# The first of seven products in one 512-column matmul per weight block, in the 12 pairs that follow a Down

## The chip, the cores and the metric

The kernel runs on one core of one Trainium2 chip. The metric is device time in microseconds (us) of one execution. A core has five engines with queues of their own: PE (matmuls; its weight loads are listed as PEld), DVE (elementwise work on vectors), ACT (activations and copies), POOL and SP (here, for the most part, issuing DMAs). PE writes its sums into PSUM banks; ACT and DVE read them from there into SBUF.

## The reference

A decoder trunk of two layers on 512 tokens of width 1024, in f32. Per layer:

```python
h = x + 0.5 * swiglu(rms_norm(x, ffn1_norm[l]), ffn1_w1[l], ffn1_w3[l], ffn1_w2[l])
n = rms_norm(h, mix_norm[l])
p = n @ w_in[l]          # conv, sliding-window attention, memory attention
h = h + y @ w_out[l]
h = h + 0.5 * swiglu(rms_norm(h, ffn2_norm[l]), ffn2_w1[l], ffn2_w3[l], ffn2_w2[l])
x = rms_norm(h, final_norm[l])
```

with `swiglu(x, w1, w3, w2) = (silu(x @ w1) * (x @ w3)) @ w2` and an inner width of 2816, that is 22 blocks of 128 columns. So there are four feed-forward blocks, and the change is in the `x @ w1` and `x @ w3` of each of them.

## The kernel before, in words

**Precision.** An f32 operand is split in two parts, hi (rounded to the format that PE multiplies) and lo (what is left). A product of two f32 operands is three products of parts: weight hi by operand hi, weight hi by operand lo, weight lo by operand hi. The split of a weight tile is one ACT copy to `whi` (line 148) and one DVE subtraction to `wlo` (line 149); there are four buffers of each.

**ffn** (from line 512 on) makes one feed-forward block. The 22 column blocks of w1 and w3 are worked in four quarters, `QUARTERS = ((0, 6), (6, 6), (12, 6), (18, 4))`. In each quarter `up_pair` is called for column blocks two by two (f, f + 1), and one pair of the next quarter is made ahead; then comes the quarter's *Down*: for each of the eight blocks of the output width, matmuls of lines 180 to 182 with w2 into a bank named `mm`, and a DVE instruction of line 611 that adds it to `h`. The pairs f = 0 and 2 are made without up_pair; f = 4 is `PLAIN`, f = 6 the last branch of up_pair, and f = 8 to 20 take the branch `full`. So each quarter but the first begins, behind the Down of the quarter before, with a pair f = 8, 14 or 20; f = 10, 12 and 16, 18 follow another pair.

**up_pair** (line 363) makes a pair's two column blocks, for w1 and w3 (i = 0, 1), by a Strassen-like scheme: the contraction of 1024 is cut in two halves, the tokens in two halves of 256 (`QT`), and instead of eight products of halves there are seven (numbered j = 1 to 7), of sums of weight halves with sums of operand halves. The operand sums stand ready as `M.m[j][k]`, each a tile of 128 x 2 x 256 with hi and lo side by side. The weight tiles are `raw[i]` as loaded, `raw[i]` after two sums on DVE (line 402), `X[i]` (named `wsum`, summed by an accumulating DMA on POOL, line 372) and `z`; each is split by `unit` before use.

A product has two forms.

- `product` (line 378, matmuls on line 383): for each of four contraction blocks a matmul of 256 columns with hi and one with lo, all into the same 256 columns of a bank, then four of 256 with weight lo: 12 matmuls. The whole product stands in one half of the bank.
- `beside` (line 386, matmuls on line 391): hi and lo in one matmul of 512 columns, into the two halves of a bank, then four of 256 with weight lo into the first half: 8 matmuls. The product is the sum of the bank's halves.

In the branch `full`, `x[i]` is a bank named `pt`. Products 1, 6 and 5 go into it one on top of the other, and after each the running sum is taken to `part[i]`. For products 6 and 5 this is done by the helper `both`: `beside`, a copy of the bank's first half by ACT (line 440), and an add of its second half by DVE (line 402, `part <- part, pt`). Product 1 has the form `product`, and ACT alone takes it to `part` (line 446). Product 2 goes into a bank `po` by `beside`; `summed` adds its two halves to `part` on DVE. Products 3 (bank `cf` or `mm`), 7 and 4 (banks `po`) have the form `beside` too.

**Order.** The instructions' order on each engine is not that of the program: a planner places each by its priority and a modelled due time, allocates the buffers and sets the waits. `tc.issue_after` holds an instruction back until another is issued. Once planned, the order on an engine is fixed, and an instruction whose input is late holds what is behind it.

Of the kernel before, what the change touches and what calls it, by code (L numbers as in the profile page):

```python
# [65 lines left out]
def trunk(ctx: ExitStack, tc: tile.TileContext, xT, memT, pos, w1a, w3a, w2a, w1b, w3b, w2b,  # L66
# [293 lines left out]
        unit.at = split(p[0], p[1], x, V)[1]  # L360
        return p

    def up_pair(l, w13, f, M, full, behind=None):

        raw = [raw_tile(w13[i][l, f], D) for i in range(2)]
        X = []
        for i in range(2):

            x = wst.tile([P, UNIT], F32, tag="aux", name="wsum", bufs=3)
            with tc.issue_after(behind.ins) if behind else nullcontext():  # L370
                nc.sync.dma_start(x.rearrange("p (f c) -> p f c", f=2), w13[i][l, f : f + 2, :, 0:QW].rearrange("f p c -> p f c"))
            G.dma_start(x, w13[i][l, f + 1], accum_op=ALU.add)
            X.append(x)
        z = wst.tile([P, UNIT], F32, tag="raw", name="raw", bufs=3)
        for i in range(2):
            nc.sync.dma_start(z[:, blk(i, QW)], w13[i][l, f + 1, :, QW:])
        x0, x1 = blk(0, QT), blk(1, QT)

        def product(ps, w, half, j, first=False):


            for n, (part, q) in enumerate([(0, q) for k in range(4) for q in ((k, 0), (k, 1))] + [(1, (k, 0)) for k in range(4)]):
                tail[0] = T.matmul(ps, w[part][:, blk(4 * half + q[0])], M.m[j][q[0]][:, q[1]], skip_group_check=True,  # L383
                                   start=first and not n, stop=n == 11)

        def beside(ps, w, half, j, first=False):


            def go(out, part, n):
                for k in range(4):  # L390
                    tail[0] = T.matmul(out, w[part][:, blk(4 * half + k)], M.m[j][k][:, 0:n], skip_group_check=True,  # L391
                                       start=first and not part and k == 0, stop=part == 1 and k == 3)

            go(ps, 0, 2)
            go(ps[:, 0], 1, 1)

        u, g = (tmp.tile([P, 2, S], F32, tag=t, name=t, bufs=n) for t, n in (("u", 1), ("g", 2)))
        part = [tm("part", "sq", 2) for _ in range(2)]
        to = (u, g)

        def add(out, a, b):
            V.tensor_tensor(out=out, in0=a, in1=b, op=ALU.add)

        def summed(out, ps, a):
            add(out, ps[:, 0], a)
            add(out, out, ps[:, 1])

        if f == PLAIN:
            xy = [bank([P, S], "po") for _ in range(2)]
            zv = [bank([P, S], "pt") for _ in range(2)]  # L410
            for i in range(2):
                w = unit(raw[i])
                product(xy[i][:, x0], w, 0, 1, first=True)
                product(xy[i][:, x1], w, 1, 2)
                A.activation(part[i], xy[i], AF.Copy)
                add(to[i][:, 0, x0], part[i][:, x0], part[i][:, x1])

                add(raw[i][:, 0:QW], raw[i][:, 0:QW], X[i][:, QW:])
                add(raw[i][:, QW:], raw[i][:, QW:], raw[i][:, 0:QW])
            for i in range(2):  # L420
                w = unit(raw[i])
                product(xy[i][:, x0], w, 0, 6)
                A.activation(part[i][:, x1], xy[i][:, x0], AF.Copy)
                product(zv[i][:, x0], w, 1, 3, first=True)
            for i in range(2):
                w = unit(X[i])
                product(xy[i][:, x0], w, 1, 5)
                A.activation(part[i][:, x0], xy[i][:, x0], AF.Copy)
                product(zv[i][:, x1], w, 0, 7)
                add(to[i][:, :, x1], zv[i].rearrange("p (n t) -> p n t", n=2), part[i][:, x0].unsqueeze(1).to_broadcast([P, 2, QT]))  # L430
            w = unit(z)
            for i in range(2):
                product(zv[i][:, x1], w, i, 4)
                add(to[i][:, 1, x0], zv[i][:, x1], part[i][:, x1])
        elif full:
            x = [bank([P, 2, QT], "pt") for _ in range(2)]

            def both(i, w, half, j, t, first=False):
                beside(x[i], w, half, j, first)
                A.activation(part[i][:, t], x[i][:, 0], AF.Copy)  # L440
                add(part[i][:, t], part[i][:, t], x[i][:, 1])

            for i in range(2):
                w = unit(raw[i])
                product(x[i][:, 0], w, 0, 1, first=True)
                A.activation(part[i][:, x0], x[i][:, 0], AF.Copy)
                y = bank([P, 2, QT], "po")
                beside(y, w, 1, 2, first=True)
                summed(to[i][:, 0, x0], y, part[i][:, x0])
            c, v = [bank([P, 2, QT], t) for t in ("cf", "mm")], []  # L450
            for i in range(2):
                with tc.issue_after(unit.at.ins):
                    add(raw[i][:, 0:QW], raw[i][:, 0:QW], X[i][:, QW:])
                add(raw[i][:, QW:], raw[i][:, QW:], raw[i][:, 0:QW])
                w = unit(raw[i])
                both(i, w, 0, 6, x1)
                beside(c[i], w, 1, 3, first=True)
                w = unit(X[i])
                v.append(bank([P, 2, QT], "po"))
                beside(v[i], w, 0, 7, first=True)  # L460
                A.activation(to[i][:, 1, x1], v[i][:, 0], AF.Copy)
                add(to[i][:, 1, x1], to[i][:, 1, x1], v[i][:, 1])
                both(i, w, 1, 5, x0)
                summed(to[i][:, 0, x1], c[i], part[i][:, x0])
                add(to[i][:, 1, x1], to[i][:, 1, x1], part[i][:, x0])
            w = unit(z)
            for i in range(2):
                beside(v[i], w, i, 4)
                summed(to[i][:, 1, x0], v[i], part[i][:, x1])
        else:  # L470
            x = [bank([P, QT], "pt") for _ in range(2)]
            for i in range(2):
                w = unit(raw[i])
                product(x[i], w, 0, 1, first=True)
                A.activation(part[i][:, x0], x[i], AF.Copy)
                y = bank([P, 2, QT], "po")
                beside(y, w, 1, 2, first=True)
                summed(to[i][:, 0, x0], y, part[i][:, x0])

                add(raw[i][:, 0:QW], raw[i][:, 0:QW], X[i][:, QW:])  # L480
                add(raw[i][:, QW:], raw[i][:, QW:], raw[i][:, 0:QW])
            c, v = [bank([P, 2, QT], t) for t in ("cf", "mm")], []
            for i in range(2):
                w = unit(raw[i])
                product(x[i], w, 0, 6)
                A.activation(part[i][:, x1], x[i], AF.Copy)
                beside(c[i], w, 1, 3, first=True)
            for i in range(2):
                w = unit(X[i])
                v.append(bank([P, 2, QT], "po"))  # L490
                beside(v[i], w, 0, 7, first=True)
                A.activation(to[i][:, 1, x1], v[i][:, 0], AF.Copy)
                add(to[i][:, 1, x1], to[i][:, 1, x1], v[i][:, 1])
                product(x[i], w, 1, 5)
                A.activation(part[i][:, x0], x[i], AF.Copy)
                summed(to[i][:, 0, x1], c[i], part[i][:, x0])
                add(to[i][:, 1, x1], to[i][:, 1, x1], part[i][:, x0])
            w = unit(z)
            for i in range(2):
                beside(v[i], w, i, 4)  # L500
                summed(to[i][:, 1, x0], v[i], part[i][:, x1])
        out = gated()
        for n, sign in enumerate((1.0, -1.0)):
            A.activation(u[:, n], u[:, n], AF.Silu, scale=sign)
        M.gated = V.tensor_tensor(out=g, in0=g, in1=u, op=ALU.mult)
        for n, sign in enumerate((1.0, -1.0)):
            hi, lo = out[n]
            A.activation(hi, g[:, n], AF.Copy, scale=sign)  # L508
            V.scalar_tensor_tensor(out=lo, in0=g[:, n], scalar=sign, in1=hi.bitcast(F32), op0=ALU.mult, op1=ALU.subtract)  # L509
        return out  # L510

    def ffn(l, w13, w2, x, sums, factors, last, at_product, aside=None, closing=None):
# [70 lines left out]
        for q, (f0, nf) in enumerate(QUARTERS):  # L583
            ahead = 2 if q + 1 < len(QUARTERS) else 0
            for f in range(f0, f0 + nf + ahead, 2):
                if f not in g:
                    g[f], g[f + 1] = up_pair(l, w13, f, M, f > QUARTERS[1][0], behind if f < QUARTERS[1][0] else None)
                    if f == PLAIN:
                        with tc.issue_after(M.gated.ins):
                            rescale = after()  # L590
# [793 lines left out]
```

## Time and profile before

| | us |
|---|---|
| median of three runs (lowest to highest) | 1751.56 (1750.62 to 1752.01) |
| the profiled execution | 1751.12 |
| its span, first to last instruction | 1749.3 |
| PE busy in it | 1735.9 |
| DVE busy in it | 1398.0 |
| ACT busy in it | 904.4 |

The granted PE clock is 0.998 of full speed over the span. In rows of the profile, `out<-in` names the tiles, `x12` is a count, and the shapes are partitions x elements. A row in order of time begins with its start and its length in us, and ends, where the engine sat idle before it, with that idle time and what ended it in brackets; rows of like instructions are merged. Matmuls overlap, so the time that one takes from PE is the distance from its start to the next start. A row of waits has the sum in us, the count and the longest.

### The profile page before, as it was taken

Reading aid. Unit: us, or ns where it says so; the run is one execution under the profiler, and the core shown is the slowest. Engines: PE = TensorE matmul, PEld = TensorE weight load, DVE = VectorE, ACT = ScalarE, POOL = GpSimd, SP = SyncE. Lnnn points to the kernel's source line nnn. Section 1 sums busy time; section 2 is a strip of 40 time slices with the busy share of each in tenths; the row PEclk is TensorE's granted clock in tenths of the full one; section 3 lists DMA queues with packets and bytes.
Section 4 is the critical chain, followed back from the end, with each engine's and each line's share of the span. In section 5 each row is a group of like instructions: output and inputs, shape, how many; then the busy total and the mean of one; then the engine's idle time right before and its main releaser. Section 6 shows DMA issues by size and latency. Waiting matters only on the chain.

```text
span 1749.3 us, 25622 instructions
## 1 busy us (share of the span) xinstructions
PE 1735.9 (99%) x9556; PEld 1499.7 (86%) x9556; DVE 1398.0 (80%) x2330; ACT 904.4 (52%) x1437; POOL 193.9 (11%) x220
## 2 busy tenths in 40 slices
PE   9999999999999999999999999999999999999998
PEld 7988888888888988888889888888888889888886
DVE  7968789889877869686778796968898768696966
ACT  6635354555765535353655353535567655353533
POOL 1000000006121000000010000000251310000000
PEclk9999999999999999999999999999999999999999
DMA  8456565357247546464566474643671666474622
GB/s 276 128 140 178 135 166 147 103 160 169 82 93 184 137 131 175 136 177 137 154 146 169 123 185 118 176 140 106 169 161 49 145 145 181 124 186 127 171 79 85
DMA packets 96332, 253.43 MB, mean 145 GB/s; under 512 B 9808, under 2 KB 16208, under 8 KB 96208
## 3 DMA queue, kind: packets, MB, share of 16 engines
q1 hardware_dynamic: 77200, 190.45, 34.1%
q0 software_dynamic: 19008, 61.35, 20.1%
q8 instruction: 75, 1.23, 0.3%
q14 instruction: 49, 0.40, 0.1%
HBM read 249.67 MB, written 2.10 MB: 144 GB/s over the span
## 4 chain that ended last, share of the span: by engine, by line
PE 96%; DVE 2%; ACT 1%; DMA 1%; issue 0%; SPq 0%; DVEq 0%; ACTq 0%
PE po L391 15%; PE mm L180 14%; PE mm L182 14%; PE mm L181 14%; PE pt L391 9%; PE pt L383 8%; PE mm L391 2%; PE cf L391 2%; PE po L383 2%; PE po L180 2%; PE po L182 2%; PE po L181 2%; PE po L989 2%; PE mm L937 1%; PE cf L180 1%; PE cf L182 1%
## 5 line engine op out<-in xcount | busy, mean ns | idle before, releaser
L148 ACT ACTIVATE whi<-raw 128x1024 fp32r<-128x1024 f32 (+3 forms) x346 | 326.1, 948 | 434.0 <-PE mm L181 204.0
L149 DVE TENSOR_TENSOR wlo<-raw,whi 128x1024 fp32r<-128x1024 f32 (+3 forms) x346 | 374.3, 1090 | 70.9 <-ACT whi L148 51.6
L180 PE MATMUL mm<-ghi,whi 128*128 128x512 f32 (+1 forms) x752 | 292.1, 390 | 0.7 <-ACT ghi L508 0.4
L181 PE MATMUL mm<-glo,whi 128*128 128x512 f32 (+1 forms) x752 | 292.3, 389 | 0.0
L182 PE MATMUL mm<-ghi,wlo 128*128 128x512 f32 (+1 forms) x734 | 285.2, 389 | 0.0
L611 DVE SCALAR_TENSOR_TENSOR h<-mm,h 128x512 f32<-128x512 f32 x126 | 86.6, 690 | 139.4 <-PE mm L182 139.1
L180 PEld LDWEIGHTS mm<-ghi,whi 128*128 128x128 f32 x752 | 141.1, 188 | 30.6 <-ACT ghi L508 1.3
L181 PEld LDWEIGHTS mm<-glo,whi 128*128 128x128 f32 x752 | 141.2, 188 | 28.0 <-DVE glo L509 0.4
L182 PEld LDWEIGHTS mm<-ghi,wlo 128*128 128x128 f32 x734 | 137.8, 188 | 27.9
L391 PE MATMUL po<-xlo,whi 128*128 128x512 f32 x512 | 139.5, 394 | 0.0
L1119 DVE SCALAR_TENSOR_TENSOR there<-ypad,par,there 128x512 f32<-128x512 f32 x180 | 136.2, 781 | 1.3
L180 PE MATMUL mm<-xhi,whi 128*128 128x512 f32 x256 | 101.8, 398 | 0.0
L391 PEld LDWEIGHTS po<-xlo,whi 128*128 128x128 f32 x512 | 89.4, 188 | 13.3
L181 PE MATMUL mm<-xlo,whi 128*128 128x512 f32 x256 | 99.6, 389 | 0.0
L182 PE MATMUL mm<-xhi,wlo 128*128 128x512 f32 x256 | 99.5, 390 | 0.0
L148 ACT ACTIVATE whi<-wsum 128x1024 fp32r<-128x1024 f32 x72 | 75.7, 1051 | 33.8 <-PE mm L181 30.2
L149 DVE TENSOR_TENSOR wlo<-wsum,whi 128x1024 fp32r<-128x1024 f32 x72 | 87.8, 1219 | 2.7 <-ACT whi L148 2.7
L391 PEld LDWEIGHTS po<-xlo,wlo 128*128 128x128 f32 x512 | 78.2, 188 | 10.8
L391 PE MATMUL po<-xlo,wlo 128*128 128x256 f32 x512 | 81.3, 280 | 0.0
L440 ACT ACTIVATE part<-pt 128x256 f32<-128x256 f32 x112 | 42.0, 375 | 61.0 <-PE pt L391 61.0
L383 PE MATMUL pt<-mh,whi 128*128 128x256 f32 x512 | 71.7, 283 | 0.0
L383 PEld LDWEIGHTS pt<-mh,whi 128*128 128x128 f32 x512 | 66.6, 191 | 1.0
(410 smaller groups left out, 3659.8 us busy)
## 6 DMA issues: line engine op xcount, KB each, us to landing
raw<-in_w2a SPq DMA_DIRECT2D x48, 384.0 KB, 3.7
raw<-in_w2b SPq DMA_DIRECT2D x48, 384.0 KB, 3.8
raw<-in_w1a SPq DMA_DIRECT2D x26, 512.0 KB, 3.5
raw<-in_w3a SPq DMA_DIRECT2D x26, 512.0 KB, 3.7
raw<-in_w1b SPq DMA_DIRECT2D x26, 512.0 KB, 3.5
raw<-in_w3b SPq DMA_DIRECT2D x26, 512.0 KB, 4.0
wsum<-in_w1a SPq DMA_DIRECT2D x18, 512.0 KB, 6.6
wsum<-in_w3a SPq DMA_DIRECT2D x18, 512.0 KB, 3.8
```

Of the source, the lines that this page charges most:

```text
L148: a = A.activation(hi, x, AF.Copy)
L149: return a, on.tensor_tensor(out=lo, in0=x, in1=hi.bitcast(F32), op=ALU.subtract)
L180: T.matmul(ps, a[0], b[0], start=first, stop=False, **more)
L181: T.matmul(ps, a[0], b[1], start=False, stop=False, **more)
L182: tail[0] = T.matmul(ps, a[1], b[0], start=False, stop=last, **more)
L383: tail[0] = T.matmul(ps, w[part][:, blk(4 * half + q[0])], M.m[j][q[0]][:, q[1]], skip_group_check=True, start=first and not n, stop=n == 11)
L391: tail[0] = T.matmul(out, w[part][:, blk(4 * half + k)], M.m[j][k][:, 0:n], skip_group_check=True, start=first and not part and k == 0, st ...
L440: A.activation(part[i][:, t], x[i][:, 0], AF.Copy)
L611: added = V.scalar_tensor_tensor(out=h[:, d, :], in0=ps, scalar=0.5, in1=h[:, d, :], op0=ALU.mult, op1=ALU.add)
L937: tail[0] = T.matmul(pp[i][:, z, :], q, k, start=not masked, stop=True, skip_group_check=True)
L989: tail[0] = T.matmul(po[:, 2 * c + i, :], ptb[:, i, j, :], v, start=(j == 0), stop=(j == nk - 1))
L1119: V.scalar_tensor_tensor(out=cv[:, c, :], in0=ypad[:, c, j : j + S], scalar=conv_w[:, c, j : j + 1], in1=cv[:, c, :], op0=ALU.mult, op1=AL ...
```

## The change

`up_pair` gets an argument `ahead`. Where it is true, product 1 is made by `both`: 8 matmuls into both halves of the bank, ACT's copy of the first half, and a DVE add of the second half into `part`. ffn sets it for f - 2 equal to the quarter's first block or to 18, which in each feed-forward block is f = 8, 14 and 20. Products 6 and 5 go on top as before; they, and the sum taken after each, are unchanged.

```diff
-    def up_pair(l, w13, f, M, full, behind=None):
+    def up_pair(l, w13, f, M, full, behind=None, ahead=False):
...
             for i in range(2):
                 w = unit(raw[i])
-                product(x[i][:, 0], w, 0, 1, first=True)
-                A.activation(part[i][:, x0], x[i][:, 0], AF.Copy)
+                if ahead:
+                    both(i, w, 0, 1, x0, True)
+                else:
+                    product(x[i][:, 0], w, 0, 1, first=True)
+                    A.activation(part[i][:, x0], x[i][:, 0], AF.Copy)
                 y = bank([P, 2, QT], "po")
                 beside(y, w, 1, 2, first=True)
                 summed(to[i][:, 0, x0], y, part[i][:, x0])
...
                 if f not in g:
-                    g[f], g[f + 1] = up_pair(l, w13, f, M, f > QUARTERS[1][0], behind if f < QUARTERS[1][0] else None)
+                    g[f], g[f + 1] = up_pair(l, w13, f, M, f > QUARTERS[1][0], behind if f < QUARTERS[1][0] else None,
+                                               f - 2 in (f0, QUARTERS[-1][0]))
```

## The prediction

> **What bounds the kernel now.** I read the page first (busy shares, then the chain that ended last), then who PE waited for, then the order of time in one of the changed pairs.
>
> ```profile
> span 1749.3 us, 25622 instructions
> ...
> PE 1735.9 (99%) x9556; PEld 1499.7 (86%) x9556; DVE 1398.0 (80%) x2330; ACT 904.4 (52%) x1437; POOL 193.9 (11%) x220
> ...
> PE 96%; DVE 2%; ACT 1%; DMA 1%; issue 0%; SPq 0%; DVEq 0%; ACTq 0%
> ```
>
> PE is busy for 99% of the span and carries 96% of the chain. What is left for other engines is in the table of PE's waits:
>
> ```profile
> PE mm L554 <- ACT whi L148: 1.2, 1, 1.2
> PE pt L136 <- DVE nhalf L138: 1.1, 1, 1.1
> PE pt L1302 <- POOL rsq L197: 1.0, 1, 1.0
> ...
> PE mm L180 <- ACT ghi L508: 0.4, 2, 0.2
> ...
> PE mm L180 <- ACT whi L148: 0.3, 1, 0.3
> ```
>
> The three longest lie at the start and the end of the kernel (L136, L554, L1302). In all four feed-forward blocks together only the L180 rows touch what follows a pair, 0.7 us. No row says that PE waited for `part` or for an add of line 402, although the kernel already has 112 products of the new form, each with an add out of the bank that PE writes next (below). So the time falls by what PE saves, and rises only where the added work makes PE wait where it does not wait now.
>
> **The change on PE.** The condition is true for f = 8, 14 and 20 in each of four calls of ffn, so 12 pairs, two first products each: 24 products. Each loses 12 matmuls of 256 columns and gets four of 512 and four of 256. The moved columns are the same (12 x 256 = 4 x 512 + 4 x 256); 96 matmuls and 96 weight loads go. This is PE in the first of the 12 pairs:
>
> ```profile
> 220.18 1.11 PE L383 MATMUL pt<-mh,whi 128*128 128x256 f32 x8
> ...
> 221.62 0.63 PE L391 MATMUL po<-mh,whi 128*128 128x512 f32 x2
> ...
> 223.02 1.12 PE L383 MATMUL pt<-mh,whi 128*128 128x256 f32 x8
> ...
> 224.45 0.63 PE L391 MATMUL po<-mh,whi 128*128 128x512 f32 x2
> ...
> 225.85 1.09 PE L391 MATMUL pt<-ml,whi 128*128 128x512 f32 x4
> ...
> 230.06 1.09 PE L391 MATMUL pt<-ml,whi 128*128 128x512 f32 x4
> ...
> 231.46 1.09 PE L391 MATMUL mm<-xhi,whi 128*128 128x512 f32 x4
> ```
>
> From start to start the two old first products take 221.62 - 220.18 = 1.44 and 224.45 - 223.02 = 1.43 us. Four products of the new form stand between 225.85 and 231.46: 5.61 / 4 = 1.4025 us. A product therefore gains 1.435 - 1.4025 = 0.0325 us, and 24 gain 0.78 us. That is all of the gain, since PE has no wait here that could go. The rows have a resolution of 0.01 us, which bounds the gain between 0.02 and 0.045 us per product, 0.5 to 1.1 us in all; I take 0.78.
>
> The Trainium skill, "TensorE: Matmul & The Clock Gate", section "Wait — 56ns, not 53.3ns?", gives a warm matmul its columns at 2.4 GHz and a fixed 2.5 ns or so. By that rule, as an estimate from that page, an old product takes 12 x 109.2 = 1310 ns and a new one 4 x 215.8 + 4 x 109.2 = 1300 ns, so the 24 gain 0.24 us. The trace has both longer, 1.44 and 1.40 us, with more between them, and the measurement decides; either way the sign is the same.
>
> **The change on ACT and DVE.** ACT copies the same 128x256 half (its line becomes 440 instead of 446), so nothing is added there. DVE gets one add per product, `part <- part, pt`, of which the trace has 112:
>
> ```profile
> L402 DVE TENSOR_TENSOR part<-part,pt 128x256 f32<-128x256 f32 x112 | 45.9, 417 | 14.7 <-ACT part L440 14.5
> ```
>
> So 417 ns on its own, and where DVE goes from one add to the next, 0.33 us (228.13 to 228.46, below). 24 adds take 7.9 us at the closer pitch and 10.0 us alone. No DMA is issued, moved or passed, on SP or POOL. What hides the adds is DVE's idle time in the very pairs that get them:
>
> ```profile
> 220.20:238.50 18.30, 18.30 (x114) 16.36 (x113) 13.56 (x22) 9.09 (x14) 1.72 (x2) 1.00 0.61 165
> 238.50:256.70 18.20, 18.20 (x114) 16.28 (x113) 17.89 (x31) 11.40 (x18) 0.86 (x1) 1.00 0.72 186
> 321.00:344.00 23.00, 23.00 (x138) 20.37 (x138) 19.36 (x38) 14.64 (x28) 2.13 (x3) 1.00 0.29 79
> 1185.00:1208.00 23.00, 23.00 (x139) 20.37 (x138) 19.66 (x38) 14.82 (x28) 2.15 (x3) 1.00 0.27 81
> ```
>
> These are stretches (from:to), then length and busy time of PE, PEld, DVE, ACT and POOL. In the pair after the Down DVE is busy for 13.56 of 18.30 us, so 4.7 us are idle; the next pair has 0.3 us. Two adds make 0.67 to 0.83 us. They stay in the first pair if they come before its gaps and if each gap ends by PE's pace:
>
> ```profile
> 221.30 1.23 DVE L149 TENSOR_TENSOR wlo<-wsum,whi 128x1024 fp32r<-128x1024 f32 x1 [0.22 <-ACT whi L148]
> 222.44 0.69 DVE L402 TENSOR_TENSOR raw<-raw,wsum 128x512 f32<-128x512 f32 x1
> ...
> 225.52 1.22 DVE L149 TENSOR_TENSOR wlo<-raw,whi 128x1024 fp32r<-128x1024 f32 x1 [0.88 <-ACT whi L148]
> 226.66 0.42 DVE L402 TENSOR_TENSOR g<-po,part 128x256 f32<-128x256 f32 x1
> ...
> 228.13 0.41 DVE L402 TENSOR_TENSOR g<-g,po 128x256 f32<-128x256 f32 x1
> 228.46 0.41 DVE L402 TENSOR_TENSOR part<-part,pt 128x256 f32<-128x256 f32 x1
> 229.53 1.22 DVE L149 TENSOR_TENSOR wlo<-raw,whi 128x1024 fp32r<-128x1024 f32 x1 [0.66 <-ACT whi L148]
> ...
> 232.08 0.42 DVE L402 TENSOR_TENSOR part<-part,pt 128x256 f32<-128x256 f32 x1 [0.98 <-ACT part L440]
> 234.16 1.23 DVE L149 TENSOR_TENSOR wlo<-raw,whi 128x1024 fp32r<-128x1024 f32 x1 [1.66 <-PE pt L391]
> ```
>
> ```profile
> 221.82 0.39 ACT L446 ACTIVATE part<-pt 128x256 f32<-128x256 f32 x1 [0.55 <-PE pt L383]
> 224.43 1.06 ACT L148 ACTIVATE whi<-raw 128x1024 fp32r<-128x1024 f32 x1 [2.22 <-DVE raw L402]
> 225.39 0.36 ACT L446 ACTIVATE part<-pt 128x256 f32<-128x256 f32 x1
> ...
> 228.44 1.06 ACT L148 ACTIVATE whi<-raw 128x1024 fp32r<-128x1024 f32 x1 [0.59 <-PE cf L391]
> ```
>
> The first copy ends at 222.21, so the add can stand at 222.44, ahead of `raw <- raw, wsum`. Behind it wait that sum, the ACT split at 224.43 that takes the sum, and the second copy at 225.39: each moves 0.33 us. The second add then stands ahead of the 226.66 row, and DVE is 0.67 us late at 228.8. There the 0.66 us gap ahead of 229.53 begins; its end is set by ACT's split at 228.44, which waited for PE. The gaps of 0.98 and 1.66 us behind it end with PE too. The lag is gone by 229.5, and the nearly full second pair starts as before.
>
> The added wait is PE's: the next product into the same bank must follow the add. For bank one that is 225.85, the add done by about 222.9; for bank two 230.06, the add done by about 227.4. Both have over 2 us to spare, and I put the wait at nothing. With the cover gone, each add would cost PE its 0.33 to 0.42 us. The split made late at 225.52 serves the second 6 product, at 230.06, about 3 us behind the end of the split.
>
> Ten pairs have this pattern. In the other two (the last pairs of each layer's first feed-forward block, the windows at 321 and 1185) the memory projection shares ACT and DVE:
>
> ```profile
> 330.40 1.09 PE L391 MATMUL pt<-ml,whi 128*128 128x512 f32 x4
> ...
> 333.41 1.09 PE L391 MATMUL pt<-xhi,whi 128*128 128x512 f32 x4
> ...
> 347.98 0.73 PE L180 MATMUL mm<-ghi,whi 128*128 128x512 f32 x2 [0.21 <-ACT ghi L508]
> ```
>
> ```profile
> 328.31 0.42 ACT L446 ACTIVATE part<-pt 128x256 f32<-128x256 f32 x1
> 330.50 0.38 ACT L446 ACTIVATE part<-pt 128x256 f32<-128x256 f32 x1 [1.77 <-DVE hs L693]
> ```
>
> ```profile
> 332.42 0.42 DVE L402 TENSOR_TENSOR part<-part,pt 128x256 f32<-128x256 f32 x1 [0.34 <-ACT part L440]
> ...
> 342.48 0.69 DVE L149 TENSOR_TENSOR wlo<-raw,whi 128x512 fp32r<-128x512 f32 x1 [0.76 <-ACT whi L148]
> ```
>
> Here the first copy ends at 328.73 and PE wants the bank at 330.40, so the add has 1.25 us to be placed in; DVE has a gap of only 0.34 us until 332.42, and that add is what the matmul at 333.41 needs. The gap of 0.76 us ahead of 342.48 can take the 0.67 us before the tail that already made PE wait at 347.98. I bound the cost of these two pairs between nothing and four adds at 0.33, 1.3 us, and take nothing, because the 0.34 and 0.76 us of gaps exceed the two adds.
>
> **The sum.** The profiled execution took 1751.12 us, 1.82 more than its span of 1749.3; 1751.12 - 0.78 = 1750.34. The median of the runs, 1751.56, is 0.44 us above the profiled one, and the forecast goes by it: 1751.56 - 0.78 = **1750.8 us**. The runs lie from 1750.62 to 1752.01. What a measurement of this kernel can tell from no change is about 0.2%, 3.5 us, so below 1748.06 is faster and above 1755.06 slower.
>
> **The rivals.** *B, the two tight pairs pass their adds on.* For it: the wait at 347.98 shows that PE hangs on DVE's tail there, and ACT's 1.77 us at 330.50 shows a copy already held by a DVE instruction. Against it: the two gaps. Price 4 x 0.33 - 0.78 = +0.5, so 1752.1.
>
> *C, slower: DVE's lag is carried into the full pair behind.* The mechanism is DVE's order. If the add is queued where its copy is not done, or behind the splits of the next pair at 234.16, the gaps of the first pair are lost as waiting, and the 0.3 us that the second pair has idle don't take it up. It decides from the point where more than the 3.3 us of gaps from 228.8 to 234.2 are used up. Then all 24 adds reach PE: 7.9 - 0.78 = +7.1, so 1758.7. Against it: 112 adds of this kind wait 14.7 us in all, 0.13 us each.
>
> *D, the planner orders other things anew.* The order on each engine is planned from due times, and 24 more adds can turn a tie elsewhere. A new wait of the length of the longest that a pair now has (0.3 us, L180 on whi) in each of the 16 stretches between Downs would be +4.8 - 0.78, so 1755.6; turned the other way, only the 0.7 us of the L180 rows can be won there.
>
> *E, faster: the weight loads that go count in full.* PEld is busy for 86% of the span, and if the 96 loads were on the path, the old and new product would differ by far more. Four of the old products' matmul pitches of 0.12 us (1.44 / 12) each, 24 x 0.48 = 11.5 us, would give 1740.0. Against it stands the pitch of 1.4025 us of the new form.
>
> **How the numbers follow.** Forecast A 73%, B 12%, C 8%, D 5%, E 2%. A's own range is 1749.9 to 1751.9, the gain's bounds and the spread of the runs. The range reaches over B and its spread, 1749.5 to 1753.5, and leaves out C, most of D and E. Faster: E and 1 of A, 0.03. Slower: C and 3 of D, 0.11. Within 0.2%: the rest, 0.86.
>
> **What would show it.** PE at 9460 matmuls; L440 at 136 and L446 at 32; `part <- part, pt` at 136; a first product of 1.40 us from start to start; DVE at about 1408 us busy, with the gap ahead of the first pair's 229.53 row shrunk or gone and those behind it nearly whole; and no new row in PE's waits. A row there that names `part`, `raw` or `wlo` makes B or C right; waits far from the 12 pairs make D right. The forecast is wrong if the time moves by more than 2 us either way.

## The result, and the profile after

The changed kernel takes 1773.45 us (median of four runs, 1772.11 to 1777.51) against 1751.09 us: a ratio of the means of 1.0131, with a 95% interval of 1.0119 to 1.0143. It is slower by 22 us, and the time lies far above the forecast's range. The profiled execution took 1772.31 us, with a span of 1770.2 us.

The page of the changed kernel:

```profile
span 1770.2 us, 25425 instructions
...
PE 1741.5 (98%) x9460; PEld 1497.3 (85%) x9460; DVE 1406.4 (79%) x2354; ACT 907.0 (51%) x1437; POOL 194.0 (11%) x220
...
PE 91%; DVE 4%; DMA 2%; ACT 2%; issue 0%; SPq 0%; DVEq 0%; ACTq 0%
...
L180 PE MATMUL mm<-ghi,whi 128*128 128x512 f32 (+1 forms) x752 | 293.9, 393 | 15.7 <-ACT whi L148 14.4
...
L440 ACT ACTIVATE part<-pt 128x256 f32<-128x256 f32 x136 | 51.1, 376 | 108.4 <-PE pt L391 104.1
...
L402 DVE TENSOR_TENSOR part<-part,pt 128x256 f32<-128x256 f32 x136 | 56.0, 412 | 13.5 <-ACT part L440 13.5
```

The counts are those of the change (9460 matmuls, 136 copies on line 440, 136 adds into `part`). PE's share of the chain of waits fell from 96% to 91%. The new row is L180, the first line of a Down. The table of PE's waits says how often it waited:

```profile
PE mm L180 <- ACT whi L148: 14.4, 8, 3.0
...
PE mm L180 <- ACT ghi L511: 1.3, 4, 0.6
...
PE mm L728 <- DVE ypad L760: 0.7, 1, 0.7
...
PE pt L391 <- DVE part L402: 0.2, 1, 0.2
```

That is eight waits of 14.4 us in all, where the kernel before had one of 0.3. None is in the 12 pairs. All eight stand at the first Down matmuls behind the third pair (f = 12 and 18), some 55 us behind the changed products. The waits show in the stretches from pair f = 8 to pair f = 14 and from 14 to 20, eight in all. Six of them took 91.74 to 92.32 us before and now take 93.37 to 95.57; the two from 14 to 20 in the first feed-forward blocks took 100.35 and 100.86 and now take 102.29 and 104.20. The eight together are 17.9 us longer, the two last pairs of the first feed-forward blocks 2.0 us, the rest of the span 1.0 us. The waits make 14.4 of the 17.9; a fall of the clock behind one of them (last section) is about 1.6 more, and the rest was not followed up.

The same place, the third pair (f = 12) of the first layer, in the kernel before, in order of time on DVE, SP, POOL, ACT and PE:

```profile
170.26 1.22 DVE L149 TENSOR_TENSOR wlo<-wsum,whi 128x1024 fp32r<-128x1024 f32 x1
173.87 1.22 DVE L505 TENSOR_TENSOR g<-g,u 128x1024 f32<-128x1024 f32 x1
175.00 1.22 DVE L149 TENSOR_TENSOR wlo<-raw,whi 128x1024 fp32r<-128x1024 f32 x1
179.73 1.29 DVE L509 SCALAR_TENSOR_TENSOR glo<-g,ghi 128x512 fp32r<-128x512 f32 x2
...
171.51 0.38 SPq L371 DMA_DIRECT2D wsum<-in_w3a  x1
176.25 0.33 SPq L105 DMA_DIRECT2D raw<-in_w2a  x1
...
175.69 0.86 POOL L372 DMA_DIRECT2D wsum<-in_w3a  x1 [8.79 <-DMA wsum<-in_w3a]
...
183.65 0.50 PE L180 MATMUL mm<-ghi,whi 128*128 128x512 f32 x1 [0.31 <-ACT whi L148]
```

And in the changed kernel (its lines behind the edit have moved by 3 or 4):

```profile
171.35 1.22 DVE L149 TENSOR_TENSOR wlo<-wsum,whi 128x1024 fp32r<-128x1024 f32 x1
173.09 1.22 DVE L508 TENSOR_TENSOR g<-g,u 128x1024 f32<-128x1024 f32 x1
176.25 1.28 DVE L512 SCALAR_TENSOR_TENSOR glo<-g,ghi 128x512 fp32r<-128x512 f32 x2
178.11 1.22 DVE L149 TENSOR_TENSOR wlo<-raw,whi 128x1024 fp32r<-128x1024 f32 x1
...
172.60 0.38 SPq L371 DMA_DIRECT2D wsum<-in_w3a  x1
179.36 0.33 SPq L105 DMA_DIRECT2D raw<-in_w2a  x1
...
177.73 0.86 POOL L372 DMA_DIRECT2D wsum<-in_w3a  x1 [11.19 <-DVE glo L512]
...
184.37 0.84 ACT L148 ACTIVATE whi<-raw 128x768 fp32r<-128x768 f32 x1 [2.05 <-DMA raw<-in_w2a]
...
185.27 0.50 PE L180 MATMUL mm<-ghi,whi 128*128 128x512 f32 x1 [1.97 <-ACT whi L148]
```

Read from below: PE waits 1.97 us for ACT's split of the Down's second weight; ACT waits 2.05 us for that weight's load; SP issues the load at 179.36 instead of 176.25. The load goes into one of three `raw` buffers, which comes free with the split `wlo <- raw` of the second weight sum: 178.11 instead of 175.00. Two things stand ahead of that split on DVE. DVE is 1.1 us late (171.35 for 170.26), and the rounding of the pair before (`glo`) has changed places with the split. So the planner has put the work of pairs two and three in another order, although the edit is in the first pair alone. It has done so in the first pair too. PE's rows before and after:

```profile
133.53 1.09 PE L391 MATMUL pt<-ml,whi 128*128 128x512 f32 x4
...
134.94 1.09 PE L391 MATMUL cf<-xhi,whi 128*128 128x512 f32 x4
```

```profile
133.37 1.09 PE L391 MATMUL cf<-xhi,whi 128*128 128x512 f32 x4
...
134.54 1.09 PE L391 MATMUL pt<-ml,whi 128*128 128x512 f32 x4
```

Product 3 (bank `cf`) now stands ahead of product 6 (bank `pt`), which leaves the add more time. Three theories were put to the test: (1) the new order costs the time; (2) DVE has no room for the adds' work; (3) the new form itself costs.

### The profile page after: what moved, and what is told of

The parts are those of the page before. It is cut to its first block, busy times and chain, and to the rows that moved or that the text cites. A ratio compares the mean times of both kernels' runs of the same rounds, so it can differ in the third digit from the quotient of the medians.

```text
span 1770.2 us, 25425 instructions
## 1 busy us (share of the span) xinstructions
PE 1741.5 (98%) x9460; PEld 1497.3 (85%) x9460; DVE 1406.4 (79%) x2354; ACT 907.0 (51%) x1437; POOL 194.0 (11%) x220
## 4 chain that ended last, share of the span: by engine, by line
PE 91%; DVE 4%; DMA 2%; ACT 2%; issue 0%; SPq 0%; DVEq 0%; ACTq 0%
PE mm L180 14%; PE mm L182 14%; PE mm L181 13%; PE po L391 13%; PE pt L391 9%; PE pt L383 6%; PE po L383 2%; PE cf L391 2%; PE mm L391 2%; PE po L180 2%; PE po L182 2%; PE po L181 2%; PE po L993 2%; DMA raw<-in_w2a 1%; PE mm L941 1%; DVE wlo L149 1%
## 5 line engine op out<-in xcount | busy, mean ns | idle before, releaser
L180 PE MATMUL mm<-ghi,whi 128*128 128x512 f32 (+1 forms) x752 | 293.9, 393 | 15.7 <-ACT whi L148 14.4
L180 PEld LDWEIGHTS mm<-ghi,whi 128*128 128x128 f32 x752 | 141.2, 188 | 47.8 <-ACT whi L148 16.1
L391 PE MATMUL po<-xlo,whi 128*128 128x512 f32 x512 | 139.0, 393 | 0.0
L440 ACT ACTIVATE part<-pt 128x256 f32<-128x256 f32 x136 | 51.1, 376 | 108.4 <-PE pt L391 104.1
L180 PE MATMUL mm<-xhi,whi 128*128 128x512 f32 x256 | 101.8, 398 | 0.0
L391 PEld LDWEIGHTS po<-xlo,whi 128*128 128x128 f32 x512 | 89.2, 189 | 13.6 <-DVE u L402 0.4
L391 PEld LDWEIGHTS po<-xlo,wlo 128*128 128x128 f32 x512 | 78.4, 189 | 9.5
L391 PE MATMUL po<-xlo,wlo 128*128 128x256 f32 x512 | 84.2, 281 | 0.0
L402 DVE TENSOR_TENSOR part<-part,pt 128x256 f32<-128x256 f32 x136 | 56.0, 412 | 13.5 <-ACT part L440 13.5
L507 ACT ACTIVATE u<-u 128x512 f32<-128x512 f32 x72 | 44.0, 624 | 35.7 <-DVE u L402 35.7
```

The costliest lines, as they stand in the source:

```text
L180: T.matmul(ps, a[0], b[0], start=first, stop=False, **more)
```

## The experiments

### The form without the add, and the add without the form

`form_only` makes the first product by `beside` but leaves out the add. The hi-by-lo part of product 1 is then missing from the sums. `add_only` keeps `product` and puts a DVE add of the same shape behind it.

```diff
+                if ahead:                                   # form_only
+                    beside(x[i], w, 0, 1, True)
+                    A.activation(part[i][:, x0], x[i][:, 0], AF.Copy)
...
+                if ahead:                                   # add_only
+                    product(x[i][:, 0], w, 0, 1, first=True)
+                    A.activation(part[i][:, x0], x[i][:, 0], AF.Copy)
+                    add(to[i][:, 0, x0], part[i][:, x0], x[i][:, 0])
```

> In the 12 pairs behind a Down the first product is issued as 4 matmuls of 512 columns and 4 of 256, as in the change, but the DVE add that completes it is left out: the hi-by-lo part of the first product is not in the sums, and the order of all instructions on DVE is that of the kernel before. Theory 1 (the adds make the planner put the work in another order, and that order costs the time): the order is the old one, so only the PE gain of 24 x 0.0325 = 0.8 us is left: 1750.3 us, no wait of a first Down matmul on whi above 0.4 us. Theory 2 (DVE has no room for the adds' work and passes it on to PE): there is no add, so 1750.3 us too. Theory 3 (the 512-column form itself costs on PE or in the bank that it fills): 1760 us or more.

> The first product stays 12 matmuls of 256 columns; behind it stands a DVE add of the change's shape that reads the product's bank and writes to the pair's sum tile, where a later instruction overwrites it (so the sums are those of the kernel before). The planned order is nearly that of the changed kernel. Theory 1 (order): the whole loss and no PE gain: 1772 to 1776 us, with first Down matmuls that wait 1.3 to 3 us for whi behind the third pair of each quarter. Theory 2 (the adds' work): the same total of adds, so a loss too, 1760 to 1776 us; this run does not tell theories 1 and 2 apart, the run with adds and the old order does. Theory 3 (form): 1751 us.

`form_only`: 1751.15 us, ratio 1.0001 (0.9992 to 1.0010). `add_only`: 1773.98 us, ratio 1.0130 (1.0117 to 1.0144), with eight waits of L180 on whi, 17.2 us. Theory 3 falls: all of the loss comes with the add. The PE gain is there: with the form alone 11 of the 12 pairs are shorter, nine of them by 0.08 us. One, near 1190, is longer by 0.9 us, behind a weight load that came late in the profiled execution.

### The adds' work in the old order

`sbuf_add` keeps `product` and puts an add of the same length behind it that reads SBUF alone, so that the bank does not wait for it. `tiny_add` has the opposite: an add of 8 columns that reads the bank, a dependence with hardly any work.

```diff
+                    add(to[i][:, 0, x0], part[i][:, x0], part[i][:, x0])                 # sbuf_add
...
+                    add(to[i][:, 0, 0:8], part[i][:, 0:8], x[i][:, 0, 0:8])              # tiny_add
```

> The first product stays as before, and a DVE add of the change's shape is put behind its eviction, which adds the evicted part to itself (SBUF alone, no read of the bank; its output is overwritten later). The bank is free as early as before, and PE's planned order is nearly the old one. Theory 1 (order): 1751 to 1753 us. Theory 2 (the adds' work passes to PE): 1757 to 1761 us. Theory 3: 1751 us.

> The first product stays 12 matmuls of 256, and the DVE add behind it reads 8 columns of its bank instead of 256 (its output is overwritten later): the dependence of the bank on DVE is there, the add's work is not. The planned order has product 3 ahead of product 6 in the first pair, as the changed kernel, but the second and third pairs are nearly those of the kernel before. Theory 1a (the first pair's order alone costs): 1768 us or more. Theory 1b (the third pair's order, with the rounding ahead of the split, makes most of it): 1751 to 1758 us. Theory 2 (the adds' work): 1751 us.

`sbuf_add`: 1752.40 us, ratio 1.0010 (1.0001 to 1.0019). `tiny_add`: 1750.85 us, ratio 0.9997 (0.9988 to 1.0006). In `sbuf_add` nine of the ten common pairs cost nothing, to 0.01 us, and the tenth 0.03. What its trace has lost lies in the two last pairs of the first feed-forward blocks (1.0 and 0.5 us). So 20 of the 24 adds, those of ten pairs out of twelve, are hidden at full length, as the prediction had it. Theory 2 falls for these. `tiny_add` says less than was expected of it. Its plan turned only two matmuls of product 3 ahead of product 6, and its pairs two and three are those of the kernel before, so it shows only that the bank's dependence is harmless in that order.

### The change in the old order

`q3` is the whole change with product 3 held behind product 6 on PE. `q3_ten` is the same in ten pairs; the last pairs of the first feed-forward blocks keep their old first product.

```diff
                 both(i, w, 0, 6, x1)
-                beside(c[i], w, 1, 3, first=True)
+                with queued() if ahead else nullcontext():
+                    beside(c[i], w, 1, 3, first=True)
```

> The whole change, and one hold: in the 12 pairs product 3 is planned behind product 6 on PE, as the kernel before had it. PE's order is then the old one in the eight pairs of the quarters, and the DVE adds stand where the prediction put them; they are all done. Theory 1 (order): the loss is gone and the PE gain stays: 1750 to 1752 us, the second raw<-in_w2a of a quarter issued at about 176.3 us as before, no first Down matmul that waits over 0.7 us. Theory 2 (the adds' work): the 24 adds are there, so at least their 7.9 to 10 us stay: 1758 us or more. Theory 3: 1760 us or more.

> The change with product 3 held behind product 6, in ten of the 12 pairs: the last pairs of each layer's first feed-forward block, where the run with all twelve lost 1.9 and 2.2 us, keep their old first product. Theory 1: old order, 20 adds in DVE's gaps, 0.08 us won per pair: 1751.0 - 0.8 = 1750.2 us (1749.8 to 1750.8). If the adds have a cost that the two pairs only made visible: above 1751.5 us.

`q3`: 1754.74 us, ratio 1.0022 (1.0013 to 1.0030). `q3_ten`: 1750.78 us, ratio 0.9997 (0.9988 to 1.0006). The ten common pairs each win 0.08 to 0.09 us in `q3`, against the 0.065 of the prediction, with all their adds done. What `q3` loses, 1.9 and 2.1 us, lies in the two other pairs, and the rows point to the hold, though no run has the hold there without the adds. The kernel before had product 3 first in those two (its `cf` at 328.99 stands ahead of the `pt` at 330.40 that the prediction shows). With `cf` held back PE has nothing to do there:

```profile
330.10 0.41 PE L729 MATMUL mm<-cst,ypad 128*128 128x128 f32 x2 [1.11 <-DVE ypad L761]
330.67 1.19 PE L391 MATMUL pt<-ml,whi 128*128 128x512 f32 x4 [0.15 <-DVE part L402]
```

So the measured 1754.74 fits neither expectation. `q3_ten`, inside its expected range, leaves these two pairs out: with the change in ten pairs and the old order the time can't be told from that of the kernel before. DVE's work by stretches shows where the adds went. These are the stretches of pair one, two and three; length and busy time of PE, PEld, DVE, ACT and POOL; first the kernel before, then `q3`, then the changed kernel:

```profile
127.80:146.00 18.20, 18.20 (x112) 16.23 (x112) 13.38 (x21) 9.09 (x14) 1.73 (x2) 1.00 0.64 179
146.00:164.00 18.00, 18.00 (x112) 16.07 (x111) 17.70 (x31) 11.40 (x18) 0.86 (x1) 1.00 0.66 175
164.00:182.00 18.00, 18.00 (x112) 16.11 (x111) 17.49 (x33) 9.85 (x16) 1.72 (x2) 1.00 0.69 160
```

```profile
127.80:146.00 18.20, 18.20 (x105) 15.89 (x104) 14.05 (x23) 9.17 (x14) 1.73 (x2) 1.00 0.60 174
146.00:164.00 18.00, 18.00 (x112) 16.08 (x111) 17.69 (x31) 11.40 (x18) 0.86 (x1) 1.00 0.68 179
164.00:182.00 18.00, 18.00 (x112) 16.12 (x111) 17.49 (x33) 9.86 (x16) 1.72 (x2) 1.00 0.66 159
```

```profile
127.80:146.00 18.20, 18.20 (x105) 15.86 (x103) 13.34 (x21) 8.96 (x14) 1.72 (x2) 1.00 0.64 174
146.00:164.00 18.00, 18.00 (x113) 16.19 (x113) 17.80 (x33) 11.55 (x19) 0.86 (x1) 1.00 0.65 166
164.00:182.00 18.00, 18.00 (x109) 15.94 (x108) 17.65 (x33) 10.07 (x17) 1.72 (x2) 1.00 0.60 139
```

In `q3` the first pair does 0.67 us more on DVE and the other two are as before, to 0.01 us. In the changed kernel the first pair does no more than before. Its adds are in, but 0.7 us of other work has slipped out of it, and pairs two and three have only 0.3 and 0.5 us free. DVE is idle for 4.82 us of the first stretch before (18.20 less 13.38), 4.15 in `q3` and 4.86 in the changed kernel: in the new order the adds do not fill the gaps, which stay as waiting.

### The new order without the change

`order_only` is the kernel before, with its form and its DVE work, and product 3 put ahead of product 6 in the 12 pairs.

```diff
                 w = unit(raw[i])
+                if ahead:
+                    beside(c[i], w, 1, 3, first=True)
+                with queued() if ahead else nullcontext():
+                    both(i, w, 0, 6, x1)
+                if not ahead:
+                    beside(c[i], w, 1, 3, first=True)
```

> The form and the DVE work of the kernel before (no add, first product 12 matmuls of 256), but in the 12 pairs product 3 is given to the planner ahead of product 6, which is held behind it on PE: the changed kernel's order in the first pair without its adds. Theory 1a (the order alone costs the time): 1768 to 1775 us, with the eight waits of the first Down matmuls on whi. Theory 1b (the order takes away the gaps and the adds then fill what is left; both are needed): 1752 to 1764 us. If the order is harmless without the adds: 1751 us.

It takes 1774.14 us, ratio 1.0131 (1.0109 to 1.0154): as slow as the change, without one added instruction. PE waits at the same eight places:

```profile
PE mm L180 <- ACT whi L148: 14.1, 8, 2.2
```

That settles the first question: an order of this kind costs the time by itself. (It is not the changed kernel's order in every place: here the whole of product 3 stands ahead of product 6, there a part of it.) DVE comes to the third pair 1.5 us late, at 171.76 for the 170.26 of the kernel before, with no added work in front. What is left is which link of the order does it.

### Which link: lag, place of the split, or the buffer in the first pair

Three holds and one omission. `late_halves`: the change, with the rounding (`ghi`, `glo`) of pair two put off behind the split in pair three. `early_halves`: the kernel before, with only that split held behind the rounding. `q5`: the change, with product 7 of the second weight held behind product 5 of the first, which gives a `whi` buffer back earlier in the first pair. `less`: the change, with two DVE adds left out in pair two.

```diff
+                if i and f in (12, 18):                                                  # late_halves
+                    with tc.issue_after(unit.at.ins):
+                        up_pair.later()          # ghi and glo of the pair before
...
-                w = unit(raw[i])                                                         # early_halves
+                with tc.issue_after(up_pair.glo.ins) if i and f in (12, 18) else nullcontext():
+                    w = unit(raw[i])
...
-                beside(v[i], w, 0, 7, first=True)                                        # q5
+                with tc.issue_after(five.ins) if ahead and i else nullcontext():
+                    beside(v[i], w, 0, 7, first=True)
...
-                add(raw[i][:, QW:], raw[i][:, QW:], raw[i][:, 0:QW])                     # less
+                if f not in (10, 16):
+                    add(raw[i][:, QW:], raw[i][:, QW:], raw[i][:, 0:QW])
```

> The whole change, and one thing put off in the third pair behind a Down (f = 12 and 18): the rounding of the pair before it into ghi and glo (two ACT copies, two DVE subtractions, about 1.2 us of DVE) comes behind the split of the second weight sum instead of ahead of it. Theory 1 says that this split is the link to PE (it frees the raw buffer for the second Down weight, whose transfer the first Down matmul then waits for): the split and the issue of raw<-in_w2a come 1.2 to 1.7 us earlier, and 8 x 1.2 = 9.6 us are won back, 1762 to 1765 us. If the link is another (PE loses its time in the pairs, not at the Down): 1771 to 1774 us.

> The kernel before, unchanged in form, adds and in the order of the first and second pair behind a Down; only in the third (f = 12 and 18) the split of the second weight sum is held behind the rounding of the pair before it (glo), which is the changed kernel's order there. Theory 1, third pair: the split comes 1.2 us later or more, the second raw<-in_w2a is issued that much later, and the first Down matmuls wait 1 to 2 us in eight quarters: 1760 to 1770 us. Theory 1, lag alone: DVE is not late here, the transfer lands in time, 1751 to 1755 us.

> The whole change, with product 3 left ahead of product 6 in the 12 pairs, and one other hold on PE: product 7 of the second weight (i = 1) comes behind product 5 of the first (i = 0), as in the kernel before. In the changed kernel it stands ahead, product 5 reads the last piece of the first weight's whi 1.44 us later, and ACT's second split for the next pair waits for that buffer (142.76 instead of 141.32 us). Theory 1, buffer: this wait makes DVE's lag, which pairs two and three cannot make up, so with the hold most of the loss is gone: 1751 to 1756 us. Theory 1, third pair: the order there (the rounding ahead of the split of the second weight sum), which stays, makes the loss: 1766 us or more.

> The whole change, and less work for DVE in the second pair behind a Down: at f = 10 and 16 the second half of each weight sum is left out (two adds of 0.6 us on SBUF in each of 8 pairs; the sums of these pairs are then not the reference's). Theory 1, lag: DVE's lag of 0.5 to 1.4 us ends in the second pair, the loads for the Down start as early as before, and nearly all of the loss is gone: 1749 to 1755 us. If the wait at the Down does not come from DVE's lag but from PE's own order or from DMA: 1766 us or more.

`late_halves`: 1770.42 us, ratio 1.0104 (1.0089 to 1.0120). `early_halves`: 1757.22 us, ratio 1.0033 (1.0020 to 1.0046). `q5`: 1778.71 us, ratio 1.0161 (1.0135 to 1.0187). `less`: 1756.53 us, ratio 1.0031 (1.0020 to 1.0041).

`q5` fells the buffer theory: the first pair ended earlier (its two last splits stand together at 141.39 as in the kernel before), and the loss grew. DVE enters pair two in time (`raw <- raw, wsum` at 143.87, 144.45 in the kernel before), waits 1.03 us for ACT's split at 164.16, and is 1.4 us late in pair three (171.62 for 170.26). So here the order of pair two makes the lag.

`less` takes 1.2 us of DVE work out of pair two, and PE's row L180 on whi is down to one wait of 0.8 us; its time is just above the range that the lag theory gave. It can't tell the two links apart, though. DVE is in time again (169.95 for 170.26), and the planner has also put the third pair's split back ahead of the rounding (175.03 and 179.76). Of the 4.1 us that its trace still loses, 1.9 lie in the two last pairs of the first feed-forward blocks; the rest was not followed up.

The other two runs lie in none of their expected ranges, and they seem to disagree: with the split 1.0 us earlier only 3 us are won, within the spread of its runs, and with the split as late as in the changed kernel only 6 us are lost. The trace has the reason. The Down's weight shares the DMA engines with another transfer, the accumulating DMA of line 372 that POOL issues for a weight sum. DVE's lag moves this one too. The accumulate follows the plain load of the same `wsum`, which SP issues when DVE's split of the old `wsum` is done: at 172.60 for 171.51, to land at 177.18 for 175.14. (POOL's row of the changed kernel names `glo`; but POOL's wait ended at 177.24, with that landing, and `glo` at 177.53.) The table has means over the eight quarters, in us from the start of the first pair on PE, of the issue and the landing of both, from the trace's DMA events; last the sum of PE's waits of L180 on whi:

```
                accumulate        Down's 2nd weight   PE's
                issued  landed    issued  landed      waits
before           48.31   54.88     48.38   52.34       0.3
q3               48.13   54.98     48.30   52.34       0.3
less             47.98   54.37     48.49   53.34       0.8
early_halves     48.19   53.74     51.68   55.03       4.6
late_halves      49.70   56.32     50.37   56.27      14.1
order_only       50.22   55.88     51.50   56.38      14.1
q5               49.58   55.32     51.35   56.34      15.7
after            49.69   55.22     51.57   56.40      14.4
```

PE is ready for this weight at 55.5 (185.27 - 1.97 - 127.78), and 0.9 us pass from the landing through ACT's split to PE; so it must land by 54.6. The changed kernel's mean of 56.40 is 1.8 us late, and 8 x 1.8 = 14.4. In the kernel before the weight is issued together with the accumulate and passes it in seven of the eight quarters. In the first, whose rows stand above, it is issued 0.55 us behind, lands 0.2 us behind, and there the kernel has its one wait of 0.3. In the changed kernel it is issued 1.9 us behind the accumulate and lands 1.2 us behind it.

So the late accumulate is the heavier link. With the split behind the rounding alone (`early_halves`) the load is late, but the accumulate is nearly done by then: 4.6 us of waits. With DVE late and the rounding out of the way (`late_halves`) the accumulate is late, and the load, 0.7 us behind it, waits for its end all the same: 14.1 us, nearly the whole. That run does not have the lag quite alone: its split comes 2.1 us later than before (177.09 for 175.00), 1.3 of it lag (171.54 for 170.26), the rest other work that now stands ahead of it.

## Why the prediction was wrong

**The gain on PE** was right. The first products take 1.38 and 1.41 us from start to start, `form_only` and `q3` show 0.08 us for most pairs against the 0.065 of the prediction.

**The adds in DVE's gaps** were right for the old order, and the order was the mistake. In `q3` the gaps that the prediction named behave as it said. In the twin of the pair it read, the gap ahead of the third split shrinks from 0.66 to 0.49 us, those of 0.98 and 1.66 us stay, and the next pair starts as before:

```profile
137.21 1.23 DVE L149 TENSOR_TENSOR wlo<-raw,whi 128x1024 fp32r<-128x1024 f32 x1 [0.49 <-ACT whi L148]
...
139.76 0.42 DVE L402 TENSOR_TENSOR part<-part,pt 128x256 f32<-128x256 f32 x1 [0.98 <-ACT part L440]
141.85 2.36 DVE L149 TENSOR_TENSOR wlo<-raw,whi 128x1024 fp32r<-128x1024 f32 x2 [1.66 <-PE pt L391]
```

**The step that failed** is the sentence "The lag is gone by 229.5, and the nearly full second pair starts as before". It put the adds into the order that stood, while the planner makes the order anew. With it fell "No DMA is issued, moved or passed": the Down's second load was issued at 179.36 for 176.25, behind the accumulate. The two splits for the next pair, which end the first pair, stand back to back in `q3` (the last row above); in the changed kernel a wait has come between them:

```profile
141.24 1.22 DVE L149 TENSOR_TENSOR wlo<-raw,whi 128x1024 fp32r<-128x1024 f32 x1 [0.77 <-ACT whi L148]
143.85 1.22 DVE L149 TENSOR_TENSOR wlo<-raw,whi 128x1024 fp32r<-128x1024 f32 x1 [1.39 <-ACT whi L148]
```

**Rival D** (the planner orders other things anew) was the right one and was priced too low: 16 stretches at 0.3 us, the longest wait that a pair had. It was eight waits of 1.8 us. A bound could have been had from the rows: the Down's second weight landed at 54.80 in the first quarter (176.25 + 6.4 - 127.86), with nothing left over, since PE waited 0.31 us for it. It stands behind a split on DVE in the third pair, which has 0.5 us free behind a pair with 0.3, so a lag of DVE there goes through to PE, or more than through where the load loses its turn to another. The prediction followed each add to the next product into its bank, but not to the buffers that DVE's splits give back and the loads that wait for them.

**Rival C** had the place right and part of the mechanism: gaps of the first pair stay as waiting, and a lag goes into the full pairs. What it had wrong is the way to PE and the price. It charged the adds' own work, 7.9 us; the lag came to PE by late transfers, 1.8 us a quarter, and `order_only` has the loss without adds. **Rival B**: the two tight pairs lose 2.0 us together in the changed kernel and 1.5 in `sbuf_add`, near its 1.3. The wait on an add, which the prediction put at nothing, occurs once in the changed kernel, in one of these two: the 0.2 us of `PE pt L391 <- DVE part L402`. **Rival E** is out: with 96 weight loads fewer and no add, `form_only` saved no more than the 0.08 us per pair.

The forecast's own test, "waits far from the 12 pairs make D right", named the case.

## What to carry to other kernels

Where a planner orders the instructions, a small edit is not local: ask what the order would be with it, and which waits near zero (here 0.31 us) hold only in the present order. Follow a late engine through the buffers that it gives back to the loads behind them; a transfer that slips behind another can cost more than its own delay. If an edit is right and its order wrong, hold one instruction in its old place; here one hold won back 19 of the 22 us, and all of them with two tight pairs left out, though the edit was then worth nothing that can be measured.

## What the runs showed of the hardware that was not expected

**Two transfers are mostly served one behind the other.** The load of 384 KB lands 3.0 us after its issue when it is alone (601.28 in the kernel before). Over 13 kernels and eight quarters each, 104 cases, it lands 3.0 to 4.1 us after its issue in each of the 49 cases where it is issued before, or at most 0.47 us behind, POOL's issue of the 512 KB accumulate, and then 2.5 to 5.1 us ahead of the accumulate's end. From 0.55 us behind (54 cases) it lands after the accumulate's end, 0.2 to 2.6 us after it; the one case between them, at 0.52 us, lands 1.5 us ahead of it, after 4.8 us. The DMA queues in three stretches of the changed kernel, 179.4 to 181, 181 to 182 and 182 to 183 us (q0 is POOL's, q1 is SP's; packets, MB, share), with the load issued at 179.36:

```profile
q0 software_dynamic: 45, 0.18, 87.9%
...
q0 software_dynamic: 54, 0.22, 111.1%
...
q1 hardware_dynamic: 55, 0.17, 48.1%
q0 software_dynamic: 36, 0.09, 47.2%
```

SP's queue moves nothing until 182.26, when POOL's transfer nears its end. Where the load is served first, its first packet moves 0.9 to 1.0 us after its issue; so here it stood some 2 us behind the other queue.

Near ties go otherwise. In 13 of the 14 cases from 0.55 to 0.93 us behind, 62 to 94% of the accumulate's bytes move between the load's first packet and its landing; from 0.94 us on (40 cases) it is at most 10%. The first quarter of the kernel before (0.55 us behind) is one of the 13; the two queues from 179 to 181 us:

```profile
q0 software_dynamic: 73, 0.30, 74.6%
q1 hardware_dynamic: 67, 0.21, 28.3%
```

The Trainium skill, "DMA: Bandwidth & Descriptors", section "Queues, rings and completion order", has each DMA engine take turns between the queues that have work for it, and drain a whole packet, typically of 9 to 17 descriptors, before it turns to the next. In the trace a transfer is 144 records (128 of data, 16 of 4 bytes), which makes nine for each of 16 engines. If such nine are one packet in that sense, the service one behind the other agrees; if each record is one, the near ties agree. No run here shows which holds, or why there are both kinds.

**The clock falls after a wait of about 2 us, now and then.** Behind the wait of 1.93 us at 1060.04 the changed kernel's matmuls came at 0.43 us for some 3 us; behind the one of 3.02 us at 280.32 they did not. Length, busy times and the granted clock (the column ahead of the last two), around the wait of 3.02 us in the first row and that of 1.93 us in the other two:

```profile
280.40:284.00 3.60, 3.60 (x16) 2.97 (x17) 1.85 (x4) 0.77 (x2) 0.00 (x0) 1.00 0.41 112
1057.00:1060.00 3.00, 1.11 (x8) 0.81 (x6) 1.60 (x4) 0.98 (x3) 0.00 (x0) 1.00 0.93 304
1061.00:1064.00 3.00, 3.00 (x9) 2.32 (x8) 0.97 (x3) 0.63 (x1) 0.86 (x1) 0.50 0.99 309
```

Between the first and the last 20 us of the 13 traces the clock fell 14 times, to 0.50 for 3.41 us each, behind waits of 1.75 to 3.03 us, and never in the eight kernels that have no wait over 1.4 us there. By an estimate from these rows each fall costs about 1.6 us (eight matmuls at 0.43 for 0.23). The runs of the five kernels with such waits spread over 5 to 12.5 us, those of the others over 1.5 to 3.5, and the slower ones have the lower clock: 0.991 in the slowest run of `q5` (1786.11 us), 0.997 in its fastest (1774.12). The Trainium skill, "TensorE: Matmul & The Clock Gate", section "What's actually happening", lets the clock go to half after an idle window of about 3.4 us. The size of the fall agrees (0.50); the idle time here was shorter (1.75 to 3.03 us), and the measurement decides. What decides whether a wait ends in a fall was not tried.
